# Weight parts prepared in the first feed-forward: buffers of their own, and for most only the second part stored

## The chip, the cores and the metric

One core of one Trainium2 chip runs the whole step. The metric is device time in microseconds (us) of one launch. TensorE multiplies, VectorE (DVE), ScalarE (ACT) and GpSimd (POOL) compute beside it, and transfers issued by SyncE (SP) run on 16 DMA engines.

## The reference, cut to what matters

Two layers of a decoder trunk, for 256 prompt tokens and 8 x 4 sample tokens together, all in float32. The even layer mixes tokens by pooling and retention, the odd layer by a spatial gate and a convolution; each mixer has one input and one output projection and each layer a feed-forward:

```
z = rms(h) @ w_in;   y = concat(mixer_1(z), mixer_2(z)) @ w_out;   h = h + rms(y)
f = square(relu(rms(h) @ w_up)) @ w_down;                          h = h + rms(f)
```

With a width of 2048 and a hidden width of 8192, nearly all the arithmetic is products of the 288 token columns with float32 weights.

## The kernel before, in words

**Tiles.** Activations lie transposed, 128 channels by 288 tokens. The weights are cut into 720 *subs*, each 256 rows by 512 columns (512 KB), in the order in which they are used (`ORDER`). A group of 8 subs (4 in the odd output projection) fills four PSUM banks. Subs 0 to 111 are the even mixer, 112 to 367 the first feed-forward, 368 to 431 the input projection of the odd mixer, 432 to 463 its output projection, 464 to 719 the second feed-forward.

**Two parts.** TensorE takes a shorter number than float32, so every weight is split: `whi` is the weight rounded (ScalarE, `emit_hi`), `wlo` the rest (VectorE, `emit_lo`: raw minus `whi`). `emit_mm` then runs 24 matmuls per sub: `whi` and `wlo` by the first part of the activations, `whi` by the second.

**Kept subs.** In the odd mixer VectorE has a convolution to do as well. So 60 of the subs used there and at the start of the second feed-forward are split ahead of time, as *jobs* at subs 1 and 5 (`JOBS`) of the groups of the first feed-forward: a job's raw is loaded and split, both parts are written to DRAM (`put_out`), and where the sub is used both come back by DMA (`kept` in `emit_hi`). Of the odd mixer's other groups every second sub is kept.

**Order of the work.** `plan` writes one list, `feed`, with the subs in order and each job behind the sub of its slot. Everything walks this list by hand. Raws lie in 4 buffers (`RAW`); `fetch` issues the load of a raw as far as four raws ahead, and its DMA waits until the split of the raw that lay in the buffer is done. Split parts lie in a ring of slots: 3 in pool `wp` and 1 or 2 more in `W["pool"]` (`more_ring`), 5 in the first feed-forward, 4 in the odd mixer. The first part of a sub therefore waits on ScalarE until TensorE has finished the sub that lay in its slot. In one step of `run`, for the sub now multiplied, there come in this order: `put_out` for a job of the step before, `feed_hi` (up to two places of the list further, `some(2)`), `feed_lo`, the matmuls, and at a group's end the reading of the four banks by VectorE (`g.evac`). All instructions of an engine run in the order in which they were written; the same holds for SP's queue of transfers.

**The convolution.** `conv_all` (VectorE, `cacc`) and `conv_pool` (ScalarE's `tap`, added on GpSimd) run as fillers: `bg_step(fills)` puts in as many of their instructions per step as a count of each engine's load admits (`room`, 2.95 us taken off per sub). When both are through, `conv_out` normalises, and the second half of the output projection uses its result.

**PSUM.** Outside the odd mixer five banks go round, so the first bank of a group is free early and the second is the one that waits for VectorE; in the odd mixer there are four, since the convolution holds one.

Of the kernel before, what the change touches and what calls it, by code (L numbers as in the profile page):

```python
# [178 lines left out]
def build(tc, ctx, I, O, C):  # L179
# [34 lines left out]
    def f(ap):  # L214
        return ap.bitcast(F32)
# [258 lines left out]
    RAW, RING = 4, 3  # L474
    JOBS = (1, 5)
    raws, his = {}, {}
# [15 lines left out]
    def emit_dma(p):  # L492
        kind, i = feed[p]
        if kind == "kept":
            return
        g, s = subs[i]
        raw = wp.tile([128, 2, 512], F32, tag="raw", name="raw", bufs=RAW)
        r0, r1 = g.rows[2 * s], g.rows[2 * s + 1]
        assert r1 == r0 + 1 and ORDER[i] == (*g.w, r0, tuple(g.pieces))
        for k in range(0 if p else 2):  # L500
            SP.dma_start(out=raw[:, k, :], in_=I["wt"][i, :, k, :])
        if p:
            SP.dma_start(out=raw, in_=I["wt"][i])
        raws[p] = raw
# [7 lines left out]
    def emit_hi(p):  # L512
        kind, i = feed[p]
        hi, lo = parts[p] = ring_slot()
        if kind == "kept":
            for a, b in zip((hi, lo), kept[i]):
                SP.dma_start(out=f(a), in_=b)
        else:
            A.activation(out=hi, in_=raws[p], func=AF.Copy)
        if kind != "job":  # L520
            his[i] = hi, lo

    def emit_lo(p):
        kind, i = feed[p]
        hi, lo = parts.pop(p)
        if kind != "kept":
            V.tensor_tensor(out=lo, in0=raws.pop(p), in1=f(hi), op=SUB)
        if kind == "job":
            kept[i] = [dram.tile([128, 2, 512], F32, tag=f"{t}{i}", name=f"{t}k") for t in ("hi", "lo")]
            W["out"] = [(b, a) for a, b in zip((hi, lo), kept[i])]  # L530

# [4 lines left out]
    def plan():  # L536

        todo = []
        where = {}
        at = 0  # L540
        for gi, g in enumerate(groups):
            for s in range(g.nsub):
                subs.append((g, s))
                if g.ahead and g.ahead(s):
                    todo.append(at + s)
            where[gi] = at
            at += g.nsub
        slots = [where[gi] + s for gi, g in enumerate(groups) if g.jobs for s in g.jobs]
        assert len(slots) >= len(todo)
        slots = dict(zip(slots, todo))  # L550
        ahead = set(todo)
        for i in range(len(subs)):
            pos.append(len(feed))
            feed.append(("kept" if i in ahead else "sub", i))
            if i in slots:
                feed.append(("job", slots[i]))
        n = 0
        for kind, i in feed:
            nraw.append(n)
            n += kind != "kept"  # L560
        nraw.append(n)
# [19 lines left out]
    def some(n):  # L581

        return min(W["split"] + n - 1, pos[W["now"]] + RING + W["extra"] - 1)

# [65 lines left out]
    def run():  # L650
# [3 lines left out]
        for i, (g, s) in enumerate(subs):  # L654
# [29 lines left out]
            if last:  # L684
                if g.defer:
# [5 lines left out]
                    def rest(g=g):  # L691
                        yield from finish_pre(g.ready)
                        for m in range(0 if g.keep else 4):
                            g.evac(m, y(m))
# [25 lines left out]
    def to_ffn():  # L720
        if E["stack"]:
            E["stack"].close()
            E["stack"] = None
        else:
            Q["stack"].close()
            less_ring()
        more_ring(2)


    def ffn(layer, last):  # L730
        wu, wd = ("w_up", layer), ("w_down", layer)
        for q in range(4):
            for gm in range(4):
                def ev_up(m, ps, gm=gm):
                    k = gm * 4 + m
                    u = W["pool"].tile([128, T], F32, tag="u", name="u", bufs=8)
                    V.scalar_tensor_tensor(out=u, in0=ps, scalar=0.0, in1=rb, op0=ALU.max, op1=MUL)
# [7 lines left out]
                def st_up(q=q, gm=gm):  # L745
                    if gm == 0:
# [4 lines left out]
                                  start=st_up, kouter=first, defer=first, jobs=() if last or first else JOBS,  # L751
                                  ahead=(lambda s: True) if last and first else None))
            for gm in range(4):
# [13 lines left out]
                def fin_dn(q=q, gm=gm):  # L767
                    if q == 3 and gm == 3:
                        for m in range(4):
# [6 lines left out]
                                  post=to_odd if q == 3 and gm == 1 and not last else None,  # L776
                                  jobs=() if last or (q == 3 and gm == 3) else JOBS))

# [713 lines left out]
    def odd():  # L1492
# [9 lines left out]
        def ga(j):  # L1502
            def post_ga():
                if j == 1:
                    bg_drain(st_["setup"])
                if j == 0:
                    while "begun" not in Q:
# [8 lines left out]
                              start=odd_open if j == 0 else None, post=post_ga, kouter=j == 0, defer=j == 0,  # L1516
                              ahead=lambda s: j == 0 or s % 2 == 1))

        def vgrp(gm):
            def post_v():  # L1520
                if gm == 1:
# [4 lines left out]
                              lambda m, ps: ev_v_odd(m, ps, gm), start=start_v_odd if gm == 0 else None,  # L1526
                              post=post_v, ahead=lambda s: s % 2 == 1))

        def ugrp(gm):
            def post_u():  # L1530
                if gm == 1:
                    bg_drain(st_["gate"])

                    def tail():
                        while any(c in bgs or c in fills for c in st_["conv"]):
# [6 lines left out]
            groups.append(Grp(w, [(512 * gm, 512)], list(range(KT)), xs, lambda m, ps: ev_u(m, ps, gm),  # L1542
                              start=start_u if gm == 0 else None, post=post_u, ahead=lambda s: s % 2 == 1))

        for fn, i in ((ga, 0), (ga, 1), (ga, 2), (vgrp, 0), (vgrp, 1), (ga, 3), (ugrp, 0), (ugrp, 1)):
            fn(i)
        for half in range(2):
            for gm in range(4):
# [14 lines left out]
                def post_o(gm=gm, half=half):  # L1563
                    if half == 0 and gm == 3:
                        for c in st_["conv"]:
# [12 lines left out]
                                  before={0: hold_ring} if half == 0 and gm == 3 else None,  # L1578
                                  ahead=lambda s: s % 2 == 1))

# [129 lines left out]
```

## Time and profile before

| | |
|---|---|
| time, median of 3 runs | 2472.33 us (2472.2 to 2473.88) |
| time of the profiled execution | 2476.82 us |
| span of the profiled execution | 2475.1 us |
| TensorE matmul busy | 2420.7 us (98%) |
| VectorE, ScalarE, GpSimd busy | 1360.7, 1090.6, 251.9 us |
| granted TensorE clock, mean | 0.988 of full speed |
| moved by DMA | 529.35 MB, 214 GB/s |

The span runs from the first to the last instruction on the core; the time of an execution is a little longer. Busy matmuls overlap, so the 98% is not a share of the peak: the rate is read from the number of matmuls in a stretch. A wait row says which engine and line waited for which, how long in all, how often and the longest. The granted clock is 1.00 at full speed (2.4 GHz) and 0.50 at the lower level (1.2 GHz).

### The profile page before, as it was taken

Reading aid. Unit: us, or ns where it says so; the run is one execution under the profiler, and the core shown is the slowest. Engines: PE = TensorE matmul, PEld = TensorE weight load, DVE = VectorE, ACT = ScalarE, POOL = GpSimd, SP = SyncE. Lnnn points to the kernel's source line nnn. Section 1 sums busy time; section 2 is a strip of 40 time slices with the busy share of each in tenths; the row PEclk is TensorE's granted clock in tenths of the full one; section 3 lists DMA queues with packets and bytes.
Section 4 is the critical chain, followed back from the end, with each engine's and each line's share of the span. In section 5 each row is a group of like instructions: output and inputs, shape, how many; then the busy total and the mean of one; then the engine's idle time right before and its main releaser. Section 6 shows DMA issues by size and latency. Waiting matters only on the chain.

```text
span 2475.1 us, 43388 instructions
## 1 busy us (share of the span) xinstructions
PE 2420.7 (98%) x17976; PEld 2386.2 (96%) x17976; DVE 1360.7 (55%) x1844; ACT 1090.6 (44%) x1567; POOL 251.9 (10%) x293
## 2 busy tenths in 40 slices
PE   9999999999999999999999999899999999999997
PEld 8899999999999999999999999899999999999997
DVE  5665564764455556555546976346434544544453
ACT  5343443554544455455434443435434434433442
POOL 0521111000000000000114750100000000000011
PEclk9999999999999999999999999999999999999998
DMA  7555464588888888888775656455555554545552
GB/s 253 164 185 181 159 206 160 181 280 296 289 289 297 279 295 290 294 288 293 261 254 211 246 200 219 179 196 190 168 164 168 163 169 161 172 162 170 165 166 92
DMA packets 146871, 529.35 MB, mean 214 GB/s; under 512 B 16809, under 2 KB 17849, under 8 KB 146649
## 3 DMA queue, kind: packets, MB, share of 16 engines
q1 hardware_dynamic: 142240, 511.81, 60.4%
q0 software_dynamic: 4288, 14.71, 1.8%
q8 instruction: 140, 2.29, 0.4%
q14 instruction: 59, 0.48, 0.1%
q10 hardware_dynamic: 144, 0.07, 0.0%
HBM read 453.68 MB, written 73.87 MB: 213 GB/s over the span
## 4 chain that ended last, share of the span: by engine, by line
PE 84%; DVE 6%; DMA 4%; ACT 3%; issue 2%; SPq 0%; POOL 0%; DVEq 0%; ACTq 0%; POOLq 0%
PE mm L604 81%; DVE wlo L162 2%; DVE cacc L162 2%; DMA raw<-in_wt 2%; DMA wlo<-lok 1%; ACT whi L162 1%; ACT tmp L162 1%; PE ms L313 1%; DMA lok<-wlo 1%; PE po L995 1%; DVE tmp L162 1%; PE ms L999 0%; DVE conv L162 0%; DVE yo L162 0%; PE ms L303 0%
## 5 line engine op out<-in xcount | busy, mean ns | idle before, releaser
L162 DVE TENSOR_TENSOR wlo<-raw,whi 128x1024 fp32r<-128x1024 f32 (+1 forms) x721 | 886.9, 1240 | 751.1 <-ACT whi L162 737.3
L162 ACT ACTIVATE whi<-raw 128x1024 fp32r<-128x1024 f32 (+1 forms) x721 | 755.1, 1057 | 1011.2 <-PE mm L604 892.1
L604 PE MATMUL mm<-xhi,wlo 128*128 128x288 f32 x3200 | 944.9, 297 | 11.3 <-DVE wlo L162 9.2
L604 PE MATMUL mm<-xhi,whi 128*128 128x288 f32 x3200 | 944.2, 297 | 10.3 <-DVE tmp L162 6.2
L604 PE MATMUL mm<-xlo,whi 128*128 128x288 f32 x3200 | 919.6, 296 | 0.0
L604 PE MATMUL mm<-hidhi,whi 128*128 128x288 f32 x2560 | 754.8, 296 | 6.8 <-ACT whi L162 3.2
L604 PE MATMUL mm<-hidhi,wlo 128*128 128x288 f32 x2560 | 757.6, 297 | 2.5 <-DMA wlo<-lok 1.7
L604 PE MATMUL mm<-hidlo,whi 128*128 128x288 f32 x2560 | 745.2, 296 | 0.0
L604 PEld LDWEIGHTS mm<-xhi,wlo 128*128 128x128 f32 x3200 | 605.4, 189 | 16.0 <-DVE wlo L162 13.2
L604 PEld LDWEIGHTS mm<-xhi,whi 128*128 128x128 f32 x3200 | 605.9, 189 | 13.3 <-issue 6.8
L604 PEld LDWEIGHTS mm<-xlo,whi 128*128 128x128 f32 x3200 | 595.8, 189 | 0.5 <-DVE xlo L162 0.5
L604 PEld LDWEIGHTS mm<-hidhi,whi 128*128 128x128 f32 x2560 | 485.3, 190 | 8.1 <-ACT whi L162 3.4
L604 PEld LDWEIGHTS mm<-hidhi,wlo 128*128 128x128 f32 x2560 | 485.4, 190 | 3.3 <-DMA wlo<-lok 2.1
L604 PEld LDWEIGHTS mm<-hidlo,whi 128*128 128x128 f32 x2560 | 480.3, 189 | 0.0
L162 POOL TENSOR_TENSOR acc<-acc,tmp 128x288 f32<-128x288 f32 x55 | 53.3, 970 | 1657.1 <-ACT tmp L162 1654.3
L162 DVE TENSOR_TENSOR y<-mm,y 128x288 f32<-128x288 f32 x112 | 50.9, 457 | 103.3 <-PE mm L604 103.3
L162 DVE SCALAR_TENSOR_TENSOR u<-mm,rb 128x288 f32<-128x288 f32 x120 | 54.3, 457 | 71.2 <-PE mm L604 71.2
L162 DVE SCALAR_TENSOR_TENSOR cacc<-gx,vecs,cacc 128x256 f32<-128x256 f32 x168 | 68.5, 478 | 0.0
L162 ACT ACTIVATE hidhi<-u 128x288 fp32r<-128x288 f32 x128 | 56.9, 445 | 4.1
L162 ACT ACTIVATE u<-u 128x288 f32<-128x288 f32 x128 | 55.3, 432 | 7.0 <-DVE u L162 6.9
L162 POOL TENSOR_TENSOR conv<-conv,tap 128x256 f32<-128x256 f32 x60 | 53.7, 895 | 13.6 <-ACT tap L162 10.0
L162 DVE TENSOR_TENSOR hidlo<-u,hidhi 128x288 fp32r<-128x288 f32 x128 | 49.7, 450 | 0.0
(180 smaller groups left out, 909.8 us busy)
## 6 DMA issues: line engine op xcount, KB each, us to landing
raw<-in_wt SPq DMA_DIRECT2D x719, 512.0 KB, 4.2
hik<-whi SPq DMA_DIRECT2D x60, 512.0 KB, 6.4
lok<-wlo SPq DMA_DIRECT2D x60, 512.0 KB, 7.1
whi<-hik SPq DMA_DIRECT2D x60, 512.0 KB, 4.4
wlo<-lok SPq DMA_DIRECT2D x60, 512.0 KB, 5.8
s0t<-in_state_ret POOLq DMA_DIRECT2D x24, 256.0 KB, 3.3
out<-s0t POOLq DMA_DIRECT2D x24, 256.0 KB, 3.4
out<-yo SPq DMA_DIRECT2D x8, 288.0 KB, 2.4
```

What stands on the lines that cost most here:

```text
L162: return call(*args, **kw)
L313: PE.matmul(P["sums"][:, t:t + 1], lhsT=a[:, c:c + 128], rhs=ones[:, 0:1], start=first and t == 0, stop=last and t == 2)
L604: PE.matmul(ps, lhsT=lhsT[:, k, c], rhs=rhs, start=s == 0 and k == 0 and which == 0, stop=s == g.nsub - 1 and k == 1 and which == 2)
L995: PE.matmul(po[gq:gq + 32, 0:256], lhsT=E["qdm"][:, hh, 32 * (b + i):32 * (b + i + 1)], rhs=s[:, i, :], start=False, stop=b >= 4, tile_pos ...
```

## The change

Four things are changed together.

- A kept sub is of kind `both` or `lo`. Of a `both` sub (all 8 of the odd mixer's first group and all 8 of the second feed-forward's first group) both parts go to DRAM and come back, as before. Of a `lo` sub only the second part does; the raw is loaded again where it is used and ScalarE rounds it there (`emit_hi`), so VectorE has nothing to do for it. Now all the subs of the odd input projection behind the first group are `lo`.
- A job no longer takes a slot of the ring. It splits into buffers of its own in `W["pool"]`, one `jhi` and two `jlo`. To make room the ring of the first feed-forward has 4 slots instead of 5 and `u` 4 buffers instead of 8 there; a `flush` before the second reading of a group in `rest` goes with that.
- The slots are subs 3, 5 and 7 of a group instead of 1 and 5, and none in the last three groups of the first feed-forward.
- `some` counts its limit in subs instead of places of the list.

```
-    JOBS = (1, 5)
+    JOBS = (3, 5, 7)
...
     def emit_hi(p):
         kind, i = feed[p]
-        hi, lo = parts[p] = ring_slot()
-        if kind == "kept":
-            for a, b in zip((hi, lo), kept[i]):
-                SP.dma_start(out=f(a), in_=b)
+        if kind == "job":
+            parts[p] = [W["pool"].tile([128, 2, 512], F32R, tag=t, name=t, bufs=n) for t, n in (("jhi", 1), ("jlo", 2))]
+            A.activation(out=parts[p][0], in_=raws[p], func=AF.Copy)
+            return
+        hi, lo = parts[p] = his[i] = ring_slot()
+        if kind == "both":
+            SP.dma_start(out=f(hi), in_=kept[i][0])
         else:
             A.activation(out=hi, in_=raws[p], func=AF.Copy)
-        if kind != "job":
-            his[i] = hi, lo
+        if kind != "sub":
+            SP.dma_start(out=f(lo), in_=kept[i][-1])

     def emit_lo(p):
         kind, i = feed[p]
         hi, lo = parts.pop(p)
-        if kind != "kept":
-            V.tensor_tensor(out=lo, in0=raws.pop(p), in1=f(hi), op=SUB)
+        raw = raws.pop(p, None)
+        if kind in ("sub", "job"):
+            V.tensor_tensor(out=lo, in0=raw, in1=f(hi), op=SUB)
         if kind == "job":
-            kept[i] = [dram.tile([128, 2, 512], F32, tag=f"{t}{i}", name=f"{t}k") for t in ("hi", "lo")]
-            W["out"] = [(b, a) for a, b in zip((hi, lo), kept[i])]
+            out = (hi, lo) if feed[pos[i]][0] == "both" else (lo,)
+            kept[i] = [dram.tile([128, 2, 512], F32, tag=f"k{n}{i}", name=f"k{n}") for n in range(len(out))]
+            W["out"] = list(zip(kept[i], out))
...
     def some(n):
-        return min(W["split"] + n - 1, pos[W["now"]] + RING + W["extra"] - 1)
+        return min(W["split"] + n - 1, pos[min(W["now"] + RING + W["extra"], len(subs)) - 1])
...
                         yield from finish_pre(g.ready)
+                        flush()
...
             E["stack"] = None
+            more_ring(1)
         else:
             Q["stack"].close()
             less_ring()
-        more_ring(2)
+            more_ring(2)
...
-                    u = W["pool"].tile([128, T], F32, tag="u", name="u", bufs=8)
+                    u = W["pool"].tile([128, T], F32, tag="u", name="u", bufs=8 if last else 4)
...
-                                  jobs=() if last or (q == 3 and gm == 3) else JOBS))
+                                  jobs=() if last or (q == 3 and gm > 0) else JOBS))
...
-                              ahead=lambda s: j == 0 or s % 2 == 1))
+                              ahead=lambda s: "both" if j == 0 else "lo"))
...
-                                  ahead=lambda s: s % 2 == 1))
+                                  ahead=lambda s: "lo" if half == 0 and s % 2 else None))
```

The last line asks for `lo` in the first half of the odd output projection too, which would make 80 jobs. But `half` is looked up when `plan` runs, behind the loop, where it is 1. So the program holds 72 jobs (8 `both`, 56 `lo`, 8 `both`, in this order, three to a group from sub 120 on), and in the output projection no sub is kept, where before 16 were.

**Jobs on ScalarE.** In the second group with jobs (subs 128 to 135) ScalarE's rows before, where the job's first part is one more `whi` (`whi_5367` and `whi_5497` are jobs; the other rows are subs):

```order
L162 ACTIVATE whi_5362<-raw_5195 128x1024
L162 ACTIVATE whi_5367<-raw_5272 128x1024
L162 ACTIVATE whi_5402<-raw_5294 128x1024
L162 ACTIVATE whi_5432<-raw_5336 128x1024
L162 ACTIVATE whi_5462<-raw_5365 128x1024
L162 ACTIVATE whi_5492<-raw_5374 128x1024
L162 ACTIVATE whi_5497<-raw_5406 128x1024
```

and with the change:

```order
L162 ACTIVATE jhi_5332<-raw_5163 128x1024
L162 ACTIVATE whi_5337<-raw_5197 128x1024
L162 ACTIVATE whi_5372<-raw_5272 128x1024
L162 ACTIVATE jhi_5402<-raw_5298 128x1024
L162 ACTIVATE whi_5407<-raw_5335 128x1024
L162 ACTIVATE whi_5442<-raw_5344 128x1024
L162 ACTIVATE jhi_5472<-raw_5376 128x1024
```

A job now stands two subs behind the last one, where before it was four, and all three write the one `jhi` buffer.

**The writes on SP.** The same jobs in SP's queue with the change (`k0` is the first part's place in DRAM, `k1` the second's):

```order
L503 DMA raw_5335<-in_wt 128x1024
L503 DMA raw_5344<-in_wt 128x1024
L539 DMA k0_5341<-jhi_5332 128x1024
L539 DMA k1_5342<-jlo_5333 128x1024
L503 DMA raw_5376<-in_wt 128x1024
L503 DMA raw_5405<-in_wt 128x1024
L503 DMA raw_5414<-in_wt 128x1024
L539 DMA k0_5411<-jhi_5402 128x1024
```

`raw_5335` goes into the buffer that the job's own raw leaves and `raw_5344` into that of the sub behind the job, so the write of `jhi` stands behind the splits of both.

**VectorE in the odd mixer.** The third group (subs 384 to 391), before, up to its reading of the banks (`tmp<-mm`):

```order
L162 TENSOR_TENSOR wlo<-raw,whi 128x1024
L162 TENSOR_REDUCE conv<-prod 128x32
L162 TENSOR_SCALAR conv<-conv,vecs 128x32
L162 SCALAR_TENSOR_TENSOR cacc<-gx,vecs,cacc 128x256 x9
L162 TENSOR_TENSOR wlo<-raw,whi 128x1024
L162 SCALAR_TENSOR_TENSOR cacc<-gx,vecs,cacc 128x256 x15
L162 TENSOR_TENSOR tmp<-mm,rb 128x288 x3
```

and with the change:

```order
L162 SCALAR_TENSOR_TENSOR cacc<-gx,vecs,cacc 128x256 x18
L162 SCALAR_TENSOR_TENSOR conv<-gx,vecs,cacc 128x256
L162 SCALAR_TENSOR_TENSOR cacc<-gx,vecs,cacc 128x256
L162 TENSOR_TENSOR conv<-cacc,conv 128x256
L162 TENSOR_SCALAR cacc<-gx,vecs 128x256 x2
L162 SCALAR_TENSOR_TENSOR cacc<-gx,vecs,cacc 128x256 x7
L162 TENSOR_TENSOR tmp<-mm,rb 128x288 x3
```

The splits are gone there and the filler has moved up into their place: the convolution's last sum stands in the last group of the input projection instead of the second group of the output projection, and `conv_out` begins 7 subs earlier.

## Rows read from the trace of the kernel before

**Rows 1.** The chain that ended last, shares of the span by engine (the page).
```profile
PE 84%; DVE 6%; DMA 4%; ACT 3%; issue 2%; SPq 0%; POOL 0%; DVEq 0%; ACTq 0%; POOLq 0%
```

**Rows 2.** Windows, weight matmuls alone: stretch, length, PE and PEld busy, clock, DMA share, GB/s.
```profile
700.00:1200.00 500.00, 500.00 (x3784) 500.00 (x3783) 1.00 0.83 287
464.70:548.80 84.10, 79.36 (x579) 78.00 (x578) 0.98 0.79 273
1268.30:1640.10 371.80, 326.80 (x2305) 319.69 (x2305) 0.95 0.61 222
```

**Rows 3.** Waits of PE from 1240 to 1645 us: total, times, longest.
```profile
PE mm L604 <- DVE tmp L162: 8.3, 4, 3.0
...
PE ms L1439 <- DVE mb L162: 2.9, 1, 2.9
```

**Rows 4.** Waits of PE from 1575 to 1589 us.
```profile
PE mm L604 <- ACT whi L162: 3.2, 1, 3.2
PE mm L604 <- DMA wlo<-lok: 1.2, 1, 1.2
PE mm L604 <- DVE wlo L162: 0.9, 1, 0.9
PE mm L604 <- DMA whi<-hik: 0.5, 1, 0.5
```

**Rows 5.** Window of a clock dip: PE, PEld, DVE, ACT, POOL busy, clock, DMA.
```profile
1356.50:1359.90 3.40, 3.40 (x16) 3.40 (x15) 3.30 (x7) 0.00 (x0) 1.74 (x4) 0.50 0.00 0
```

**Rows 6.** The chain that ended last, ahead of 1355.7 us: start, us, what.
```profile
1349.27 5.88 DVE cacc L162 x15
1355.15 0.37 DVE tmp L162
```

**Rows 7.** VectorE's groups from 1268.3 to 1640.1 us.
```profile
L162 DVE SCALAR_TENSOR_TENSOR cacc<-gx,vecs,cacc 128x256 f32<-128x256 f32 x168 | 68.5, 478 | 0.0
L162 DVE TENSOR_TENSOR wlo<-raw,whi 128x1024 fp32r<-128x1024 f32 x44 | 62.2, 1418 | 70.9 <-ACT whi L162 70.9
```

**Rows 8.** Waits of PE from 1304 to 1309 us.
```profile
PE mm L604 <- DMA whi<-hik: 1.3, 1, 1.3
PE mm L604 <- DMA wlo<-lok: 0.8, 1, 0.8
```

**Rows 9.** The page's groups of instructions: a split's two halves, and `hidhi`.
```profile
L162 DVE TENSOR_TENSOR wlo<-raw,whi 128x1024 fp32r<-128x1024 f32 (+1 forms) x721 | 886.9, 1240 | 751.1 <-ACT whi L162 737.3
L162 ACT ACTIVATE whi<-raw 128x1024 fp32r<-128x1024 f32 (+1 forms) x721 | 755.1, 1057 | 1011.2 <-PE mm L604 892.1
...
L162 ACT ACTIVATE hidhi<-u 128x288 fp32r<-128x288 f32 x128 | 56.9, 445 | 4.1
```

**Rows 10.** Timeline of VectorE from 766 to 775 us: start, us, what.
```profile
769.01 2.36 DVE L162 TENSOR_TENSOR wlo<-raw,whi 128x1024 fp32r<-128x1024 f32 x2 [1.95 <-ACT whi L162]
772.18 1.22 DVE L162 TENSOR_TENSOR wlo<-raw,whi 128x1024 fp32r<-128x1024 f32 x1 [0.81 <-ACT whi L162]
```

**Rows 11.** Timeline of SP's queue from 766 to 775 us.
```profile
773.81 0.64 SPq L534 DMA_DIRECT2D hik<-whi  x1
```

**Rows 12.** DMA issues from 700 to 1200 us: KB each, median us from issue to landing.
```profile
raw<-in_wt SPq DMA_DIRECT2D x195, 512.0 KB, 4.9
hik<-whi SPq DMA_DIRECT2D x39, 512.0 KB, 6.4
lok<-wlo SPq DMA_DIRECT2D x39, 512.0 KB, 7.0
```

**Rows 13.** Timeline of VectorE from 466 to 492 us.
```profile
472.01 2.35 DVE L162 TENSOR_TENSOR wlo<-raw,whi 128x1024 fp32r<-128x1024 f32 x2
...
485.63 0.15 DVE L162 TENSOR_SCALAR sm<-ms 128x3 f32<-128x3 f32 x1
```

**Rows 14.** Timeline of ScalarE from 466 to 492 us.
```profile
490.39 1.06 ACT L162 ACTIVATE whi<-raw 128x1024 fp32r<-128x1024 f32 x1 [2.07 <-DMA hik<-whi]
```

**Rows 15.** Line 303, the spread, from 480 to 500 us: ns, starts.
```profile
L303 PE MATMUL ms<-cg,sm x6: 195/274/276, 489.8 to 490.3; 128*128 128x128 f32 x4, 128*128 128x32 f32 x2
```

More of the change, by code (lines that the diff above doesn't have):

```diff
@@ L513, in emit_hi @@
         kind, i = feed[p]
-        hi, lo = parts[p] = ring_slot()
-        if kind == "kept":
-            for a, b in zip((hi, lo), kept[i]):
-                SP.dma_start(out=f(a), in_=b)
+        if kind == "job":
[3 more added lines that the diff above has]
+        hi, lo = parts[p] = his[i] = ring_slot()
+        if kind == "both":
+            SP.dma_start(out=f(hi), in_=kept[i][0])
         else:
             A.activation(out=hi, in_=raws[p], func=AF.Copy)
-        if kind != "job":
-            his[i] = hi, lo
+        if kind != "sub":
+            SP.dma_start(out=f(lo), in_=kept[i][-1])
     def emit_lo(p):
@@ L536, in plan @@
     def plan():
-        todo = []
+        todo, kinds = [], {}
         where = {}
@@ L543, in plan @@
                 subs.append((g, s))
-                if g.ahead and g.ahead(s):
+                kind = g.ahead(s) if g.ahead else None
+                if kind:
                     todo.append(at + s)
+                    kinds[at + s] = kind
             where[gi] = at
@@ L550, in plan @@
         slots = dict(zip(slots, todo))
-        ahead = set(todo)
         for i in range(len(subs)):
             pos.append(len(feed))
-            feed.append(("kept" if i in ahead else "sub", i))
+            feed.append((kinds.get(i, "sub"), i))
             if i in slots:
@@ L559, in plan @@
             nraw.append(n)
-            n += kind != "kept"
+            n += kind != "both"
         nraw.append(n)
@@ L751, in ffn @@
                                   start=st_up, kouter=first, defer=first, jobs=() if last or first else JOBS,
-                                  ahead=(lambda s: True) if last and first else None))
+                                  ahead=(lambda s: "both") if last and first else None))
             for gm in range(4):
@@ L1526, in vgrp @@
                               lambda m, ps: ev_v_odd(m, ps, gm), start=start_v_odd if gm == 0 else None,
-                              post=post_v, ahead=lambda s: s % 2 == 1))
+                              post=post_v, ahead=lambda s: "lo"))
         def ugrp(gm):
@@ L1542, in ugrp @@
             groups.append(Grp(w, [(512 * gm, 512)], list(range(KT)), xs, lambda m, ps: ev_u(m, ps, gm),
-                              start=start_u if gm == 0 else None, post=post_u, ahead=lambda s: s % 2 == 1))
+                              start=start_u if gm == 0 else None, post=post_u, ahead=lambda s: "lo"))
         for fn, i in ((ga, 0), (ga, 1), (ga, 2), (vgrp, 0), (vgrp, 1), (ga, 3), (ugrp, 0), (ugrp, 1)):
```

## The prediction

> **What bounds the kernel now.** The chain that ended last says it first: 84% of it is TensorE [rows 1]. The windows say at what rate. From 700 to 1200 us TensorE starts 3784 weight matmuls in 500 us, 0.1321 us each, so 3.17 us for a sub of 24 and 25.4 us for a group of 8 [rows 2]; nothing can be won there. The odd mixer, 1268.3 to 1640.1 us, starts 2305 of them in 371.8 us, where that rate would take 304.5: 67 us go to other matmuls, waits and clock [rows 2].
>
> The wait views show who is waited for there. Four times a group's first matmul waits for VectorE to empty a bank, 8.3 us in all, and once the gate's matmuls wait for it, 2.9 [rows 3]. Ahead of the longest the chain shows VectorE with 15 `cacc` in a row, 5.88 us, and only then the reading of the bank [rows 6]. From 1575 to 1589 us TensorE waits another 5.8 us (3.2 + 1.2 + 0.9 + 0.5) for parts that are late while `conv_out` is finished [rows 4]. After a wait of over 2 us the granted clock falls to 0.50 for 3.4 us, as at 1356.5 [rows 5]: 16 matmuls start in it where 26 would, so a dip costs 1.7 us.
>
> **What the odd mixer gains.** VectorE loses the splits of half the subs there; 44 cost 62.2 us, and `cacc` 68.5 for 168 [rows 7]. The filler takes the place of the splits, but it waits for nobody: a split waits for ScalarE, this for a slot, that for TensorE, and VectorE idled 70.9 us before them [rows 7]. With 41 `cacc`-like instructions at 0.41 to 0.48 us, some 19 us and the reading of banks, VectorE is through a group of 25.4 us in time. So the 8.3 us should go, with three dips (5.1); of the 2.9 I leave 0.9, and its dip goes (1.7); and since the convolution ends a group earlier, the 5.8 us go with two dips (3.4). Sum 8.3 + 5.1 + 2.0 + 1.7 + 5.8 + 3.4 = **26.3 us**. At 1304 to 1309 us TensorE waits 2.1 us for kept parts [rows 8]; the `lo` transfer of that place stands in SP's queue behind a raw that waits for ScalarE, so I leave that wait.
>
> At nothing I cost: 28 more roundings in the odd mixer (28 x 1.06 = 30 us on a ScalarE busy 1090.6 of 2475.1 us); the 16 subs of the output projection that VectorE splits again (a 1.24 us split beside a 3.17 us sub, [rows 9]); the ring of 4, which no job shares now; and the third job of a group (11 splits, 13.6 us of VectorE, per 25.4). A group with `lo` jobs moves 14 transfers of 0.524 MB, as with two jobs before. If the cover of the third job is gone, it shows as in the next part.
>
> **What the jobs cost.** A job whose first part is written holds the one `jhi` until that write has landed, and the next job's rounding waits for it on ScalarE, with the roundings of the subs queued behind it. The cycle of such a job is: rounding 1.06 [rows 9], its split and that of the sub behind it 2.36 [rows 10], since the write stands in SP's queue behind the raw that waits for the second (the write of a job at 773.81 follows the split that ran from 772.18 to 773.40, [rows 10, 11]), that raw's issue and hand-overs 0.5, landing 6.4 [rows 12]: **10.35 us**. Three jobs to a group leave 8.46. That ScalarE does wait for such a landing is seen once at 490.39, 2.07 us [rows 14]. A `lo` job frees `jhi` as soon as its split is done, so the 56 in between cost nothing.
>
> For the landing I take the row of the same transfer at the same rate of traffic; the bounds are 4.9 (a raw's, in that stretch) and 7.0 (the second of a pair) [rows 12]. The Trainium skill, "DMA: Bandwidth & Descriptors", section on the anatomy of one DMA on the SWDGE path, puts a transfer at 2.0 us and its bytes by 436 GB/s, so an estimate of 3.2 us for 512 KB. By that the cycle would be 7.2 us and no job late, and the sum would be the gains alone; the median of 39 rows, 6.4, speaks against it.
>
> *First region, jobs 0 to 8.* The rows from 472.01 to 474.36 [rows 13] are now the splits of sub 123 and of job 0; its write goes at 474.8 and lands at 481.2, where job 1 starts. Job 2 starts at 491.6 and its two splits end at 495.2. Behind them on VectorE stands `sm`, now at 485.63 [rows 13], and the spread, now at 489.8 [rows 15], waits for it in front of sub 127: TensorE stands 5.6 us or more. Job 3 is held to 506 by ScalarE itself (two groups' 16 activations of 0.44, [rows 9]) and its write by VectorE to 512.1; jobs 4 to 8 then start at 518.5, 528.9, 539.2, 549.6 and 560.0 (job 8 is `lo` but waits for job 7). The second bank of the next group is read 5.15 us behind the start of the last job (rounding, three splits, 0.46), 0.79 us into the group, so that sub 144 starts at 560.0 + 4.36 = 564.4 where now it is 548.8 [rows 2]: **15.5 us** later, with four dips, 6.8.
>
> *Second region, jobs 64 to 71,* counted from the start of their first group (sub 288): job 64 starts on time at 7.4, job 65 at 18.6, then one each 10.35 to job 71 at 80.7. The group at sub 312 starts at 85.1 instead of 76.1: **8.9 us**, two dips 3.4.
>
> Cost 15.5 + 6.8 + 8.9 + 3.4 = 34.6, gain 26.3: the profiled execution's 2476.82 us becomes 2485.1. That execution lies 4.5 us over the median of the runs, 2472.33; so I forecast **2481 us**.
>
> Between the bounds of the landing: at 4.9 the cycle is 8.85, sub 144 starts 8.0 us later with three dips, the second region costs nothing, and 13.1 - 26.3 gives 2459. At 7.0 it is 18.5 + 13.2 + 11.9 = 43.6, so 2490. If half the gain is missing, 2494.
>
> **Rivals.**
> - *Faster: the jobs hardly bind.* If the write lands in 4.9 us or less, or ScalarE has more room before TensorE misses a part than the 7 us I count, the gains stand nearly alone: 2446 to 2459. For it: a write's landing is measured among as many transfers as the full rate brings, and TensorE's standing still thins them. Against it: the write goes out behind two raws in both kernels. The point from which it decides is a cycle of 8.46 us. The page's rule named above would make this the outcome. Chance 0.22.
> - *They cancel.* With a landing of 5.6 and one dip less the cost is about the gain: 2468 to 2477. Chance 0.13.
> - *Much slower: the transfers of the odd mixer bind.* A `lo` sub brings 1.05 MB. At 287 GB/s [rows 2] that is 3.65 us against 3.17, 27 us over 56 subs, and the time is 2508. Against it: 287 came at a DMA share of 0.83, so about 346 are to be had, 3.03 us. Chance 0.07; that half the gain stays out beside it, 2494, has 0.12.
>
> **How the numbers follow.** The forecast has 0.46. Slower are it, the last two and little else: 0.62 with a hundredth or two from their edges given to no change. About 0.2%, 5 us, is what a measurement of this kernel can tell from no change. Faster 0.23, same 0.15, slower 0.62. The range, 2455 to 2498, leaves out the lowest part of the first rival and the transfers; the forecast's own is 2474 to 2490.
>
> **What would show it.** Right: waits of ScalarE's `jhi` for the DMA `k0<-jhi`, some 20 to 30 us in all, only around 480 to 560 us and in the fourth quarter of the first feed-forward; TensorE waiting for `whi` and for bank readings in those two stretches and not between; sub 144 some 15 to 22 us later; then an odd mixer some 25 us shorter, without waits for `tmp`. Wrong: `jhi` waits of under 2 us each with TensorE at 0.132 us per matmul throughout, or an odd mixer in which TensorE waits for `wlo<-k0`.

## The result and the profile after

The changed kernel takes 2500.27 us (median of 4 runs, 2495.76 to 2501.29) against 2473.06 us, a ratio of 1.0107 with a 95% interval of 1.0089 to 1.0124: slower, by 27 us. The forecast of slower was right, the size was not: 2481 was foreseen and 2498 was the end of the range.

Where the time went is read from the start of each sub's first matmul in both traces (every 24th weight matmul starts a sub). Lengths in us:

| subs | before | after | after - before |
|---|---|---|---|
| 0 to 111, even mixer | 437.1 | 439.0 | +1.9 |
| 112 to 159, first feed-forward, the first `both` jobs | 162.4 | 189.0 | +26.6 |
| 160 to 303, same, `lo` jobs (the 2.5 us lie in its last group) | 457.0 | 459.5 | +2.5 |
| 304 to 359, same, the last `both` jobs | 177.7 | 188.8 | +11.1 |
| 360 to 367, boundary | 34.1 | 33.7 | -0.4 |
| 368 to 431, odd input projection | 237.3 | 219.0 | -18.3 |
| 432 to 463, odd output projection | 134.5 | 135.1 | +0.6 |
| 464 to the end | 835.0 | 835.5 | +0.5 |

They add up to 24.5, the difference of the two spans (2499.6 and 2475.1). Of the first 1.9 us, 1.7 are a stretch at half clock at 12.9 us, before any changed code; other kernels below have it or lack it in the same way.

The same stretches in the windows of the weight matmuls after (stretch, length, PE and PEld busy, clock, DMA share, GB/s), to be held against [rows 2]:

```profile
439.00:602.60 163.60, 140.54 (x961) 135.81 (x962) 0.92 0.67 227
602.60:1059.60 457.00, 457.00 (x3459) 457.00 (x3458) 1.00 0.84 290
1059.60:1149.40 89.80, 82.09 (x578) 80.26 (x578) 0.94 0.76 268
1310.00:1529.00 219.00, 207.45 (x1536) 203.92 (x1537) 1.00 0.86 307
1529.00:1664.10 135.10, 111.57 (x770) 109.94 (x768) 0.91 0.46 158
```

Between the two regions of `both` jobs, three jobs to a group run at the full rate (3459 matmuls in 457.00 us, clock 1.00), so the third job, the ring of 4 and the fewer `u` buffers cost nothing there. The input projection has no half-clock stretch left, and its 307 GB/s hold TensorE up nowhere but in the 2.5 us below.

Waits of ScalarE after, from 465 to 605 us (first row) and from 1030 to 1150 us (second): total, times, longest.

```profile
ACT jhi L162 <- DMA k<-jhi: 46.1, 7, 8.8
...
ACT jhi L162 <- DMA k<-jhi: 40.7, 7, 8.4
```

There are 14 such waits in the whole program and none between the two stretches. The timeline of ScalarE after shows how long a job holds the buffer (start, us, what, idle before it and releaser):

```profile
484.80 1.06 ACT L162 ACTIVATE jhi<-raw 128x1024 fp32r<-128x1024 f32 x1 [4.78 <-DMA k<-jhi]
...
495.08 1.06 ACT L162 ACTIVATE jhi<-raw 128x1024 fp32r<-128x1024 f32 x1 [6.66 <-DMA k<-jhi]
...
525.85 1.06 ACT L162 ACTIVATE jhi<-raw 128x1024 fp32r<-128x1024 f32 x1 [8.82 <-DMA k<-jhi]
...
571.62 1.06 ACT L162 ACTIVATE jhi<-raw 128x1024 fp32r<-128x1024 f32 x1 [7.10 <-DMA k<-jhi]
...
1118.89 1.06 ACT L162 ACTIVATE jhi<-raw 128x1024 fp32r<-128x1024 f32 x1 [8.36 <-DMA k<-jhi]
```

From 484.80 to 495.08 is one cycle, 10.28 us. Fourteen cycles end in such a wait (jobs 0, 1, 3 to 7 and 64 to 70): 10.05 to 13.59 us, mean 11.1. The last two rows are job 8 and job 71, the ends of the two chains.

Waits of TensorE after, from 439 to 602.6 us:

```profile
PE ms L303 <- POOL sm L162: 8.7, 1, 8.7
PE mm L610 <- DVE wlo L162: 6.3, 6, 1.4
PE mm L610 <- ACT whi L162: 5.2, 4, 2.2
PE mm L610 <- DVE u L162: 1.1, 2, 0.6
```

The first is the spread in front of sub 127. GpSimd is named, which runs its own small `sm` from 498.68 on, 1.76 us. But that waits for VectorE, whose timeline has the first `sm` behind the splits that waited for job 2 (GpSimd's row stands last):

```profile
496.17 1.23 DVE L162 TENSOR_TENSOR jlo<-raw,jhi 128x1024 fp32r<-128x1024 f32 x1 [6.49 <-ACT jhi L162]
497.31 1.22 DVE L162 TENSOR_TENSOR wlo<-raw,whi 128x1024 fp32r<-128x1024 f32 x1
498.44 0.15 DVE L162 TENSOR_SCALAR sm<-ms 128x3 f32<-128x3 f32 x1
...
498.68 1.76 POOL L162 TENSOR_TENSOR sm<-sm,cg 128x3 f32<-128x3 f32 x1 [62.19 <-DVE sm L162]
```

Before, `sm` ran at 485.63 [rows 13].

In the odd mixer the waits of [rows 3] are gone. What TensorE still waits for, from 1310 to 1529 us (first two rows) and from 1529 to 1664 us (the others):

```profile
PE mm L610 <- DMA wlo<-k: 2.5, 2, 1.4
PE ms L1447 <- DVE mb L162: 0.5, 1, 0.5
...
PE mm L610 <- ACT y L162: 8.8, 1, 8.8
PE ms L313 <- ACT tmp L162: 1.8, 3, 0.8
```

The wait for `mb` fell from 2.9 to 0.5 us, that for `tmp` from 8.3 to nothing. But in the output projection one wait of 8.8 us stands where several stood before [rows 4]. It is for `y`, the copy that frees a bank, and ScalarE's timeline shows what the copy stands behind:

```profile
1571.11 0.63 ACT L162 ACTIVATE tmp<-tmp,vecs 128x288 f32<-128x288 f32 x1
1571.83 0.45 ACT L162 ACTIVATE hidhi<-tmp 128x288 fp32r<-128x288 f32 x1
1572.18 0.61 ACT L162 ACTIVATE tmp<-tmp,vecs 128x288 f32<-128x288 f32 x1
1572.82 0.45 ACT L162 ACTIVATE hidhi<-tmp 128x288 fp32r<-128x288 f32 x1
1573.17 1.04 ACT L162 ACTIVATE whi<-raw 128x1024 fp32r<-128x1024 f32 x1
1576.62 0.63 ACT L162 ACTIVATE tmp<-tmp,vecs 128x288 f32<-128x288 f32 x1 [2.40 <-DVE tmp L162]
```

This is one step of `conv_out`, two tiles and one sub's rounding. From its first `tmp` to that of the next step are 5.51 us; the step after takes 5.45 again. ScalarE idles 2.40 us in each, because VectorE's part stands behind the split of that step's sub:

```profile
1574.25 1.22 DVE L162 TENSOR_TENSOR wlo<-raw,whi 128x1024 fp32r<-128x1024 f32 x1 [4.75 <-ACT whi L162]
1575.39 0.82 DVE L162 TENSOR_TENSOR hidlo<-tmp,hidhi 128x288 fp32r<-128x288 f32 x2
1576.13 0.82 DVE L162 TENSOR_TENSOR tmp<-conv,rl 128x288 f32<-128x288 f32 x2
```

`whi`, `wlo`, `hidlo`, `tmp`, `tmp` make a ring over two engines, and a sub that VectorE splits is a link of it.

### The profile page after: what moved, and what is told of

It is laid out like the page before. It is cut to its first block, busy times and chain, and to the rows that moved or that the text cites. A ratio compares the mean times of both kernels' runs of the same rounds, so it can differ in the third digit from the quotient of the medians.

```text
span 2499.6 us, 43529 instructions
## 1 busy us (share of the span) xinstructions
PE 2428.7 (97%) x17976; PEld 2391.8 (96%) x17976; DVE 1358.7 (54%) x1844; ACT 1145.2 (46%) x1623; POOL 240.1 (10%) x293
## 4 chain that ended last, share of the span: by engine, by line
PE 86%; DMA 4%; issue 4%; DVE 3%; ACT 2%; POOL 0%; SPq 0%; DVEq 0%; ACTq 0%; POOLq 0%
PE mm L610 82%; DMA k<-jhi 2%; DVE wlo L162 2%; DMA raw<-in_wt 1%; ACT whi L162 1%; ACT tmp L162 1%; DMA wlo<-k 1%; PE ms L313 1%; PE po L1003 1%; PE ms L1007 0%; ACT jhi L162 0%; DVE yo L162 0%; PE ms L303 0%; DVE hidlo L162 0%; POOL sm L162 0%
## 5 line engine op out<-in xcount | busy, mean ns | idle before, releaser
L162 ACT ACTIVATE whi<-raw 128x1024 fp32r<-128x1024 f32 (+1 forms) x705 | 741.2, 1057 | 931.5 <-PE mm L610 818.2
L162 DVE TENSOR_TENSOR wlo<-raw,whi 128x1024 fp32r<-128x1024 f32 (+1 forms) x649 | 794.6, 1231 | 664.7 <-ACT whi L162 664.0
L162 DVE TENSOR_TENSOR jlo<-raw,jhi 128x1024 fp32r<-128x1024 f32 x72 | 88.0, 1222 | 90.9 <-ACT jhi L162 90.6
L162 ACT ACTIVATE jhi<-raw 128x1024 fp32r<-128x1024 f32 x72 | 76.0, 1055 | 104.9 <-DMA k<-jhi 86.8
L162 ACT ACTIVATE u<-u 128x288 f32<-128x288 f32 x128 | 55.3, 432 | 13.9 <-DVE u L162 13.8
```

The source lines that it names most:

```text
L162: return call(*args, **kw)
```

## The experiments

All ratios are against the kernel before, run beside it. First which of the job's new conditions costs the time in the first feed-forward, then what the output projection lacks.

**Two `jhi` buffers.**

```
-... for t, n in (("jhi", 1), ("jlo", 2))]
+... for t, n in (("jhi", 2), ("jlo", 2))]
```

> The change with two jhi buffers instead of one. Theory A (the one jhi buffer, held until its write has landed, costs what was lost in the first feed-forward: 26.6 us up to sub 152 and 13.6 us up to sub 320 against before): a job then waits only for the landing of the job before the last, two cycles of 10.4 to 11.4 us shared by two buffers are 5.7 us per job where 8.46 are at hand, so all 40 us go and the time is 2458 to 2463 us, with no wait of jhi for a DMA over 2 us. Rival B (the third job of a group, the ring of 4 or the u buffers make the stalls, and the jhi waits are only where the time is noted): the time stays within 5 us of 2500.

Measured: 2463.24 us, ratio 0.996 (0.9947 to 0.9974). No wait of `jhi` for its write is left (it waits for raws, 3.5 us at most). Subs 112 to 159 take 166.1 us, 304 to 359 take 177.7 as before the change. Theory A holds, at the upper end of its range: 37 us hung on one 4 KB buffer per partition, and with a second one the change makes the kernel faster. Of the first region 3.7 us stay; the kernel that writes no first parts, below, has none of them.

**Only second parts.** Every job is `lo`, also the 16 that were `both`:

```
-  ahead=lambda s: "both" if j == 0 else "lo"))
+  ahead=lambda s: "lo"))
...
-  ahead=(lambda s: "both") if last and first else None))
+  ahead=(lambda s: "lo") if last and first else None))
```

> The change with every one of its 72 jobs of the kind that writes only the second part: the first parts of the odd mixer's first group and of the second feed-forward's first group are rounded where they are used. Theory A: no job holds jhi until a landing, so the 40 us go, 2458 to 2465 us, while three jobs to a group, the ring of 4 and the 4 u buffers stay. Rival B: within 5 us of 2500. What could be lost beside it: 16 more roundings at the two places, 17 us of ScalarE, which show as TensorE waiting for whi at subs 368 to 375 and 464 to 471.

Measured: 2458.29 us, ratio 0.9941 (0.9925 to 0.9956); subs 112 to 159 160.4 us, 304 to 359 177.7. With one `jhi` buffer, a ring of 4 and three jobs to a group nothing is lost, so rival B is out. The 16 more roundings where the parts are used cost nothing that shows: subs 368 to 375 take 27.5 us (27.1 with `both`), 464 to 471 26.3 (26.1).

**The write ahead of the raws.** One buffer, but the first part is sent right behind its rounding:

```
             A.activation(out=parts[p][0], in_=raws[p], func=AF.Copy)
+            kept[i] = []
+            if feed[pos[i]][0] == "both":
+                kept[i].append(dram.tile([128, 2, 512], F32, tag=f"k0{i}", name="k0"))
+                SP.dma_start(out=kept[i][0], in_=f(parts[p][0]))
             return
```

> The change with one jhi buffer, but the write of the first part is issued right behind its rounding, ahead of the raws that wait for the next two splits, instead of behind them. Theory A (the cycle of a job is rounding, two splits, the queue behind the raws, landing; 11.1 us measured, of which some 3.6 lie between the end of the rounding and the write): the write goes out 0.4 to 1 us behind the rounding, the cycle is 7.9 to 8.6 us against 8.46 per job, so most of the 40 us go: 2460 to 2472 us. Rival E (the landing is set by the traffic, and a write that starts earlier lands no earlier, since raws are sent behind it): the cycle stays at 10 us or more, 2485 to 2500 us.

Measured: 2464.11 us, ratio 0.9968 (0.9958 to 0.9978). The two timelines of one job in this kernel, ScalarE and SP's queue:

```profile
516.71 1.06 ACT L162 ACTIVATE jhi<-raw 128x1024 fp32r<-128x1024 f32 x1 [3.83 <-DMA k<-jhi]
...
524.37 1.06 ACT L162 ACTIVATE jhi<-raw 128x1024 fp32r<-128x1024 f32 x1 [2.69 <-DMA k<-jhi]
```

```profile
517.79 0.33 SPq L520 DMA_DIRECT2D k<-jhi  x1
```

The write follows the rounding at once (516.71 + 1.06 = 517.77), and the cycle is 7.66 us. ScalarE still waits, 3.83 us at most, and TensorE loses 5.3 us in subs 112 to 159 instead of 26.6 and none in 304 to 359. In the changed kernel 3.3 of the 11.1 us lay between the end of the rounding and the write, behind the raws; 0.5 are left in the mean. Theory A's number came and rival E is out. The landing is shorter too: where ScalarE waited for it, the next rounding follows the write's issue by 5.0 to 7.6 us, 6.0 in the mean of 11 waits, against 6.2 to 8.4, 6.8 in the mean, in the changed kernel. The Trainium skill, "DMA: Bandwidth & Descriptors", section on queues, rings and completion order, says that on each engine of a queue the pieces of its transfers are taken in the order of the ring, though a later one may finish its write first. The trace agrees as far as it goes: a write that has two raws just ahead of it lands 0.8 us later in the mean.

**The `both` jobs dealt out.** Still one buffer, but after each `both` job come two `lo` jobs:

```
+        both = [i for i in todo if kinds[i] == "both"]
+        rest_ = [i for i in todo if kinds[i] != "both"]
+        todo = []
+        while both or rest_:
+            todo += both[:1] + rest_[:2]
+            both, rest_ = both[1:], rest_[2:]
         slots = dict(zip(slots, todo))
```

> The change with one jhi buffer, but the 16 jobs whose first part is written are dealt out, one to every three jobs, so that two jobs that write only the second part follow each. Theory A: one wait of ScalarE of some 4 us in each such group (the next job comes 6.3 us after, the buffer is free after 10.4 to 11.4), which the split parts that lie ready cover; no lag adds up, so nearly all 40 us go, 2458 to 2466 us. Rival B (third job, ring of 4): within 5 us of 2500, since all groups keep three jobs. A third outcome, 2470 to 2490, would say that a single wait of 4 us already reaches TensorE and that the cover is smaller than the 7 us that the prediction counted.

Measured: 2492.2 us, ratio 1.008 (1.0066 to 1.0094). None of the three numbers came: not Theory A's, not rival B's (2495 to 2505), and not the third outcome's. The last region has no loss any more (177.7), but subs 112 to 159 take 178.1 and 160 to 303, which were clean, 473.9. ScalarE's timeline of one group in this kernel:

```profile
730.74 1.04 ACT L162 ACTIVATE jhi<-raw 128x1024 fp32r<-128x1024 f32 x1
731.69 1.04 ACT L162 ACTIVATE whi<-raw 128x1024 fp32r<-128x1024 f32 x1
733.16 1.06 ACT L162 ACTIVATE whi<-raw 128x1024 fp32r<-128x1024 f32 x1 [0.43 <-DMA raw<-in_wt]
742.35 1.06 ACT L162 ACTIVATE jhi<-raw 128x1024 fp32r<-128x1024 f32 x1 [8.13 <-DMA k<-jhi]
```

After the two roundings ScalarE stands at the next job, 3.5 us behind the `both` job, and waits out nearly the whole cycle: 8.13 us. In 11.61 us it has fed two subs, of which TensorE needs one each 3.17 us. Two kernels more test this.

> The dealt-out order of jobs that cost 19 us, and the write of the first part ahead of the raws. Theory I (that kernel lost because the whole rest of one cycle, 8 to 9 us, is waited out by ScalarE at the next slot, 2 subs or 6.35 us behind, and the parts in hand last less than the 5 us that are then missing): the cycle falls from 11.7 to some 8 us, 1.7 us are missing, no wait of jhi for a DMA is over 5 us, and TensorE shows no stall from sub 160 to 240: 2458 to 2465 us. Rival J (a first part's write costs in itself, by its traffic or by SP's time): the groups from sub 160 to 223 stay at 26 to 28.6 us, 2480 us or more.

(The dealt-out order together with the early write.) Measured: 2463.37 us, ratio 0.9949 (0.9935 to 0.9964), subs 160 to 303 at 457.0. The cycle is 7.9 us in the mean, and the longest wait of `jhi` for a transfer 4.1 us, as Theory I had it.

> The same dealt-out order with the write where the change has it, but the job whose first part is written stands in the last of the three slots (sub 7 of a group) instead of the first, so that the next job comes 4 subs or 12.7 us later. Theory I: the cycle of 11 to 11.7 us is over by then, ScalarE's waits for the write fall to 3 us or less, no stall from sub 128 to 240 by them, 2458 to 2466 us. Rival J: as before, 2480 us or more, since the number of writes, the jobs and the traffic are the same.

```
-            todo += both[:1] + rest_[:2]
+            todo += rest_[:2] + both[:1]
```

Measured: 2458.93 us, ratio 0.9933 (0.9917 to 0.995), subs 112 to 159 at 163.7, 160 to 303 at 457.0. All waits of ScalarE for that write in this kernel from 493 to 860 us:

```profile
ACT jhi L162 <- DMA k<-jhi: 5.1, 5, 1.8
```

The same jobs, writes, buffers and traffic, in another of three slots: 33 us. Theory I holds and rival J is out. With a cycle of over 11 us, what decides is whether the next job comes 2 subs (6.35 us) or 4 subs (12.7 us) later; one `jhi` is enough when the slot is chosen by it.

**`half` bound where it is written.**

```
-  ahead=lambda s: "lo" if half == 0 and s % 2 else None))
+  ahead=lambda s, half=half: "lo" if half == 0 and s % 2 else None))
```

> The change with the value of half bound where the lambda is written, so that 8 subs of the first half of the odd output projection are kept as well (80 jobs, of these 64 write only the second part). Theory C (the 16 subs that VectorE splits again lengthen the convolution's output there, which is why that stretch gained nothing): each of the four steps of 5.45 us in which ScalarE and VectorE hand tmp, hidhi, whi, wlo, hidlo to each other loses a 1.2 us split in every second one, the 9.0 us wait of sub 444 falls by 2 to 5 us with a clock dip, so 2493 to 2498 us. Rival D (the chain is ScalarE's part and the hand-overs): within 2 us of 2500.

Measured: 2488.21 us, ratio 1.0063 (1.0049 to 1.0077), 12 us under the change, more than expected. Subs 432 to 463 take 122.9 us instead of 135.1. ScalarE's timeline in this kernel, at the same steps as above:

```profile
1557.81 0.63 ACT L162 ACTIVATE tmp<-tmp,vecs 128x288 f32<-128x288 f32 x1
...
1560.86 0.63 ACT L162 ACTIVATE tmp<-tmp,vecs 128x288 f32<-128x288 f32 x1
...
1566.32 0.63 ACT L162 ACTIVATE tmp<-tmp,vecs 128x288 f32<-128x288 f32 x1 [2.40 <-DVE tmp L162]
...
1569.31 0.63 ACT L162 ACTIVATE tmp<-tmp,vecs 128x288 f32<-128x288 f32 x1
```

A step whose sub is kept takes 3.05 us, one whose sub VectorE splits 5.46. So a split costs the step not its 1.22 us but 2.4: without it VectorE makes the next `tmp` while ScalarE still rounds.

**Both mendings.** All jobs `lo` and `half` bound (80 jobs), and two buffers and `half` bound:

> All jobs of the kind that writes only the second part, and 8 subs of the output projection's first half kept as well (80 jobs). Theory C (those 8 subs are worth what their stretch gained when they alone were added, 135.1 to 122.9 us from sub 432 to 464, and 8 more jobs of this kind cost nothing): 2458.3 - 12.2 = 2446 us, 2442 to 2450. Rival D2 (80 jobs of three to a group begin to cost in the first feed-forward, or the gain was that of the jobs' shift there): 2452 us or more, with TensorE standing somewhere in subs 120 to 340.

Measured: 2450.05 us, ratio 0.9912 (0.9897 to 0.9927).

> Two jhi buffers and 8 subs of the output projection's first half kept (80 jobs, 16 of them with both parts written): what the change set out to be, with the one buffer mended. Theories A and C together: 2463.2 - 12.2 = 2451 us, 2447 to 2455. Rival D2: 2458 us or more. Against the kernel with all jobs of the other kind it should be 5 us longer, all of it in subs 120 to 160, where two buffers still left 5 us.

Measured: 2454.25 us, ratio 0.9924 (0.9909 to 0.9939). Both lie at the upper end of what A and C together gave; subs 160 to 359 are clean in both, so rival D2's cost is not there. Subs 432 to 463 take 126.4 and 127.9 us: the kept subs are worth 7 us here, not the 12.2 that they brought to the change. The 3.5 us between 122.9 and 126.4 go with the clock: in this stretch the kernel with `half` alone has it at half once, at 1571.3 us, that with all jobs `lo` three times, at 1502.8, 1537.0 and 1605.2 (last section). The two mended kernels are 4.2 us apart, where 5 were expected.

**Every second sub in the input projection.**

```
-  post=post_v, ahead=lambda s: "lo"))
+  post=post_v, ahead=lambda s: "lo" if s % 2 else None))
```

(and so in the other groups behind the first; all jobs `lo`).

> All jobs write only the second part, but in the odd input projection behind its first group only every second sub is kept, as in the kernel before (44 jobs); the output projection keeps none. Theory F (the input projection gains because VectorE has no splits there and the convolution's instructions take their place): its subs 368 to 431 take 237 us again where all kept take 219.3 and the kernel before 237.3, and the time is about 2458 + 18 = 2476 us (2470 to 2482). Rival G (it gains because a job no longer shares the ring, because some counts in subs, or because only half as many parts come from the kept copies): the stretch stays at 219 to 225 us and the time within 2458 to 2464.

Measured: 2472.18 us, ratio 1.0 (0.9991 to 1.0009); subs 368 to 431 take 236.6 us. TensorE's waits in that stretch of this kernel:

```profile
PE mm L610 <- DVE tmp L162: 11.4, 5, 3.7
PE ms L1447 <- DVE mb L162: 3.4, 1, 3.4
```

The waits of [rows 3] are back: 14.8 us, where the kernel with all jobs `lo` has 0.5, of the 17.3 by which the stretch is longer than there. A stretch at half clock at 1468.0 us, with TensorE busy for 4.30 us of it, makes some 2 more. Theory F holds: in the input projection the worth of the change is that VectorE has no splits there. The whole time is only 13.9 us longer, since the output projection takes 128.8 us here and 133.4 there.

**More of the output projection kept.** 12 and all 16 subs of its first half. For 16 the edit gives four jobs to eight groups of the first feed-forward (subs 200 to 231 and 264 to 295) and leaves three to the others, where the expectation names the second and third quarter whole:

> All jobs write only the second part; of the output projection's first half 12 of the 16 subs are kept (all but each group's first; 84 jobs) where the kernel with 80 jobs kept 8. Theory C (each split that VectorE still does there stands in the hand-over between ScalarE and VectorE in which the convolution's output is made): 8 kept subs gained 7.0 to 12.2 us of subs 432 to 464, 0.9 to 1.5 each, so 4 more gain 3.5 to 6 us: 126.4 falls to 120 to 123, and 2450 to 2444 to 2447 us. Rival D (what is left of the chain there is ScalarE's own part, and the clock's dips): within 2 us of 2450.

Measured: 2450.45 us, ratio 0.9908 (0.9892 to 0.9924), subs 432 to 463 127.8 us: rival D's number. But the reason is not ScalarE's own part. VectorE's timeline of this kernel still has a split among the four steps:

```profile
1530.85 1.22 DVE L162 TENSOR_TENSOR wlo<-raw,whi 128x1024 fp32r<-128x1024 f32 x1 [2.75 <-ACT whi L162]
```

It belongs to the first sub of the next group, the only one in those steps, and the kernel with 8 leaves it too. So Theory C's count of subs was wrong and its mechanism was not: what matters is which subs fall into the steps.

> As the one with 12, but all 16 subs are kept (88 jobs; to have slots for them, the groups of the second and third quarter of the first feed-forward take four jobs each). Theory C: 8 more kept subs than with 80 jobs gain 7 to 12 us, 2438 to 2443 us. Rival H (four jobs bring 16 transfers of 0.524 MB to a group, 330 GB/s at 25.4 us where 294 were moved with three, and 12 splits of VectorE): TensorE stands in the groups with four jobs, 1 us or more in each, and the time is 2450 us or more.

Measured: 2447.16 us, ratio 0.9897 (0.9882 to 0.9912), the fastest of all, though its interval overlaps that of the kernel with 80 jobs; it lies between the two forecasts. Subs 432 to 463 take 120.5 us, 6 less, where Theory C had 7 to 12: four steps of 3 us. Windows of all the engines, 700 to 850 us, in this kernel (PE, PEld, DVE, ACT, POOL busy, clock, DMA share, GB/s), which hold the first four of the groups with four jobs:

```profile
700.00:850.00 150.00, 150.00 (x1137) 150.00 (x1136) 97.68 (x104) 81.23 (x93) 0.00 (x0) 1.00 0.89 314
```

Four `lo` jobs to a group cost nothing in these places either (1137 matmuls in 150 us, 0.1319 us each; TensorE waits nowhere from 600 to 1234 us), so rival H is out.

## Why the prediction was wrong

The sum gave 2485.1 us for a profiled execution; the profiled one took 2501.29, 16.2 more. By its own steps:

- **The output projection, "at nothing"** (9.8 us). Two steps failed together. The 16 subs that VectorE splits again were put down as "a 1.24 us split beside a 3.17 us sub", which is a busy time; the split stands in the hand-over of `conv_out` and costs its step 2.4 us. And "since the convolution ends a group earlier, the 5.8 us go with two dips (3.4)" only moved the place: the convolution's output still runs step by step with the splits, one wait of 8.8 us took the place of the 5.8, and the stretch gained -0.6 where 9.2 had been counted. With 8 of those subs kept again the stretch gains 6.6 to 11.6 on the kernel before, and with all 16 kept 14.0.
- **The price of the `both` jobs** (5.6 us: 26.6 + 2.5 + 11.1 = 40.2 where 34.6 was counted). The mechanism, its place and its number of jobs were as forecast, and the rival "the jobs hardly bind" fell. That the sum came so near is luck in part, since two larger errors cancel in it. The chains of jobs were too short: job 8 starts at 571.62, or 569.7 without the 1.9 us lost before, where 560.0 was counted, and job 71 84.7 us behind the start of sub 288, where 80.7 was counted. Against that the 10.2 us for six dips were added on top, and nothing is left for them: at the start of sub 145 and of sub 313 TensorE is 26.5 and 13.7 us later than before, and the chains alone, 15.5 + 9.7 and 8.9 + 4.0, give all but 1.3 and 0.8 of it. What made the chains longer: the wait of the spread, "5.6 us or more", was 8.7, as GpSimd's 1.8 us in front of it had been left out and job 2 came later. And the cycle, 10.35 counted, was 11.1: half of that by the way from the rounding to the write, 3.3 us for 2.36 + 0.5, half by the landing, 6.8 us by the median of its row here,

```profile
k<-jlo SPq DMA_DIRECT2D x12, 512.0 KB, 7.1
k<-jhi SPq DMA_DIRECT2D x8, 512.0 KB, 6.8
```

(issues from 470 to 605 us after), where [rows 12] had 6.4.
- **The input projection** was right: 17.1 us counted (8.3 + 5.1 + 2.0 + 1.7), 18.3 measured, and the waits for kept parts stayed, as said (2.1 then, 2.5 now).
- **"At nothing" for the third job, the 28 roundings and the ring of 4** was right, by the kernel with `lo` jobs alone.
- **The sign to look for** was too low: 20 to 30 us of `jhi` waits, where 86.8 came. ScalarE runs ahead to the next job and waits there for most of a cycle; only the part beyond its lead reaches TensorE. Sub 144 came 24.9 us later, where 15 to 22 were named.
- The remaining 1.9 us lie before the change's code, and the other stretches differ by 0.1 together. 9.8 + 5.6 + 1.9 + 0.1 - 1.2 = 16.2.

Either miss alone lay within the range: the text had 2490 for a landing of 7.0 and 2494 for half the gain missing. It had no case with both, which is why the range ended too low.

## What to carry to other kernels

A buffer that is written out belongs to its writer until the transfer has landed: compare the whole cycle (compute, what stands ahead of the write in its queue, landing) with the distance to the next user, not the mean rate of users. Where the cycle is longer, a second buffer, an earlier place in the queue, or slots with room behind them all mend it, and the slot costs no buffer. A split that is short beside a matmul may still be a link in a hand-over between two engines; cost it by the step that it lengthens, not by its busy time.

## What had not been expected of the hardware

The dips of the clock are not all alike, and not all come behind a wait. Windows of three of them after (PE, PEld, DVE, ACT, POOL busy, clock, DMA share, GB/s):

```profile
494.10:504.34 10.24, 3.85 (x17) 3.85 (x18) 4.02 (x5) 4.46 (x6) 1.76 (x1) 0.50 0.73 242
1542.00:1548.83 6.83, 6.83 (x31) 6.83 (x30) 2.64 (x5) 1.20 (x3) 0.00 (x0) 0.50 0.23 77
1586.40:1596.64 10.24, 5.76 (x24) 5.76 (x25) 3.58 (x7) 4.16 (x9) 0.00 (x0) 0.50 0.32 102
```

In a wait of some 9 us, as at 494.10 and 1586.40, the granted clock falls to 0.50 (1.2 GHz) and stays there for 10.24 us, where [rows 5] had 3.4; most of that lies inside the wait and costs nothing, since TensorE was busy for only 3.85 and 5.76 us of it (half of these, 1.9 and 2.9 us, are the price, not the 5.1 that the length alone gives). At 1542.00 it falls with TensorE busy throughout. What the engine did just before, on its timeline:

```profile
1539.90 3.36 PE L313 MATMUL ms<-cg,tmp 128*128 128x1 f32 x24 [0.44 <-ACT tmp L162]
```

24 matmuls with one column each, 3.36 us, in which it falls; then 6.83 us at half clock with 31 matmuls begun, where 52 would have been at 0.132 us each. The kernel before has such matmuls at 1540.97 and 1548.46, and its clock falls at 1544.2 and 1551.0. But they do not always bring it: in the kernel with `half` bound the same matmuls stand on TensorE's timeline, and its clock stays at 1.00 until 1571.3 us; in the kernel with all 16 kept it does so until 1601.3.

```profile
1532.91 2.73 PE L313 MATMUL ms<-cg,tmp 128*128 128x1 f32 x24
1539.75 2.84 PE L313 MATMUL ms<-cg,tmp 128*128 128x1 f32 x24 [0.83 <-ACT tmp L162]
```

Nor does a wait of over 2 us always bring a dip, as the prediction took it from the kernel before. There six waits of 2.15 to 3.17 us were each followed by one. In the kernel that keeps every second sub of the input projection three waits of 2.3 to 3.0 us were not; one of them in TensorE's timeline, and the window around it:

```profile
1353.31 0.37 PE L610 MATMUL mm<-xhi,whi 128*128 128x288 f32 x1 [2.94 <-DVE tmp L162]
```

```profile
1350.40:1356.70 6.30, 3.39 (x26) 3.42 (x27) 6.09 (x17) 1.76 (x3) 2.67 (x6) 1.00 0.42 139
```

So the dips that the prediction's gain counts with its waits are what that one execution had. Some 3 us of a run hang on the dip at 1542.00, and 1.7 on the stretch at 12.9 us; single executions of the change differ by 5.5 (2495.76 to 2501.29). That is one reason not to read less than that out of one trace. What decides where a dip comes was not tried.
